# Class 0 of the long filters begun a phase earlier, and the context filter's weights requested a row ahead

## The chip, the cores and the metric

The program runs on one core of a Trainium2 chip. Times are device microseconds (us) of one execution, from start to end on the chip; a kernel's time is the median of several executions. The core has a matrix engine (TensorE, PE in the profile; its weight loads are PEld), a vector engine (DVE), a scalar engine (ACT), a general engine (POOL) and a queue that issues transfers (SP). POOL issues transfers as well. Each engine works through its own queue of instructions in order and waits at semaphores for the others.

## What is computed

Two layers of a backbone over 1024 latent tokens (a grid of 16 by 64) and 256 context tokens, model width 1024, all in float32. Layer 0 mixes tokens by a 2-D Fourier transform on half of the channels and by an order-2 Hyena operator on the other half; layer 1 is neighbourhood attention; each ends with a SwiGLU feed-forward part. The change touches layer 0's mixer:

```python
def hyena_filters(L, w1, b1, freq, w2, b2, w3):
    ...
    h = jnp.sin(freq * (z @ w1 + b1))
    h = jnp.sin(freq * (h @ w2 + b2))
    h = (h @ w3).reshape(L, 2, HY_ORDER, HY_CH)
    ...
    h = h * jnp.exp(-t01 * deltas)[:, None, None, :]
    h = h / jnp.sum(jnp.abs(h), axis=(0, 1), keepdims=True)
    fwd, bwd = h[:, 0], h[:, 1]
    return jnp.concatenate([fwd, jnp.zeros_like(fwd[:1]), bwd[:0:-1]], axis=0)

def long_conv(u, filt, skip):
    ...
    ff = jnp.fft.rfft(filt, n=2 * L, axis=0)
    ...

def mixer_ab(u, w_in, w_out, conv_w, conv_b, w1, b1, freq, w2, b2, w3, skip):
    p = u @ w_in
    y_f = fourier_mix(p[..., :FOURIER_CH])
    y_h = hyena_mix(p[..., FOURIER_CH:], conv_w, conv_b, w1, b1, freq, w2, b2, w3, skip)
    return jnp.concatenate([y_f, y_h], axis=-1) @ w_out
```

For each of two orders there is a long filter (for the 1024 latent tokens) and a context filter (for the 256 context tokens). Both are made from the same weights w3 and turned into spectra.

## The kernel before, in words

A float32 product is made of three matmuls of a reduced type: each operand is split into a high part (a cast on ACT, L349) and a low part (a subtraction on DVE, or POOL, L351). So every operand that PE needs costs one instruction on ACT and one on DVE first.

The input projection (in_proj, L1032 on) makes p = u @ w_in in 16 rows of 128 channels, in the order 0 to 9, 12 to 15, 10, 11. Its weights come from memory one row at a time (tiles ws, split into wh and wl). Between the matmuls of one row the kernel weaves other work, the piece that belongs to the row before (the function filled): how many steps of each kind stands in a tuple of numbers per row. There are three such kinds. "long" makes the long filters, "filt" the context filters, "ada" the modulation vectors (custom DVE operations, L561).

A filter of one order is made in two parts. filter_raw requests the two halves of w3 (128x512 tiles s<-in_w, on SP), makes their sum and difference (on DVE for the long filters, on POOL, L762, for the context), splits them, and multiplies on PE with the positions' features; the product is multiplied by a window loaded from memory (L786). spectrum_l (the long filters) or spectrum_c (the context) then takes the transform as matmuls with a stored matrix (tiles tk<-in_ff_l, loaded and cast).

spectrum_l goes through four classes of frequencies in the order 2, 3, 0, 1, each in two halves p, with two operands k = 0, 1 each. An operand is a tap sum or difference of the raw filter (t tiles, from L916, L917, L955, L957, L959), split into two tiles. The generator operands runs two operands ahead of the matmuls. Classes 2 and 0 need the sums (function sums): class 0's first one needs f0, a copy of the raw filter with a corrected first row (L940 to L942). PE's results are evicted by ACT (L1000) or DVE (L1009, L1011) and stored (d<-s). Where class 0 begins, PE first makes a row sum (tile c, the matmuls ps<-s,c).

Also woven in are the Fourier half's pieces: a projected row is stored to memory (d_115 and others) and read back in another layout (s<-d; d_97 is such a tile), and DVE folds it (L1484 to L1492).

The whole program is written down in program order. A framework then takes it with its own estimate of times and its pools of tiles (35 slots "s" of the S2 kind, 6 slots "t", 8 banks of PE's accumulator memory and others) and decides the order on each engine and on SP. So code that is written earlier is not necessarily executed earlier by the same amount, and a tile's slot decides when its load may go out.

Of the kernel before, what the change touches and what calls it, by code (L numbers as in the profile page):

```python
# [16 lines left out]
MUL, ADD, SUB, MAX, MIN = ALU.mult, ALU.add, ALU.subtract, ALU.max, ALU.min  # L17
# [241 lines left out]
class Builder:  # L259
# [643 lines left out]
    def spectrum_l(self, o, raw, tot):  # L903

        nc, a = self.nc, self.a
        V = nc.vector
        classes = (2, 3, 0, 1)
        fe, fo = raw[(0, 0, 0)], raw[(0, 0, 1)]
        m0, m1, m2 = (self.mask[:, k:k + 1] for k in range(3))
        fh = []  # L910

        def sums(i, k):
# [20 lines left out]
                V.tensor_tensor(u, t, u, ADD)  # L933
            return x, u

        def operands():
            for i in classes:
                if i == 0:
                    f0 = self.f0 = self.S2()
                    V.tensor_copy(f0, fe)  # L940
                    V.tensor_tensor(f0[0:1, :], fe[0:1, :], fo[0:1, :], ADD)
                    V.scalar_tensor_tensor(f0[0:1, :], f0[0:1, :], 0.5, self.taps0[o][0:1, :], op0=MUL, op1=ADD)  # L942
                even = []
                for p in (0, 1):
                    mt = self.cast2(a["ff_l"][i, p])
                    for k in (0, 1):
                        if i % 2 == 0:
                            if p == 0:
                                even.append(sums(i, k))
                            t = even[k][p]  # L950
                        else:
                            f, r = (raw[(p + 2 * k, q, i // 2)] for q in (0, 1))
                            t = self.T()
                            if i == 1 and p + k == 0:
                                V.scalar_tensor_tensor(t, r, m1, f0, op0=MUL, op1=ADD)  # L955
                            elif p + k == 0:
                                V.scalar_tensor_tensor(t, f, m0, r, op0=MUL, op1=ADD)  # L957
                            else:
                                V.tensor_tensor(t, f, r, SUB if i == 1 else ADD)  # L959
                        xh, xl = self.S2(F32R), self.S2(F32R)  # L960
                        self.split(t, xh, xl)
                        yield xh, xl, mt[k]

        ops = operands()
        ready = [next(ops), next(ops)]
        yield
        for i in classes:
            cls, eo = i % 2, i // 2
            kept = []
            for p in (0, 1):  # L970
# [22 lines left out]
                for f in (0, 1):  # L993
# [4 lines left out]
                    if cls == 0 or p == 0:  # L998
                        t = self.S2()
# [7 lines left out]
                    elif p:  # L1007
                        x, t = self.S2(), kept[f]
# [1465 lines left out]
    def run(self):  # L2474
        nc, a = self.nc, self.a
        self.setup()
        raws = {sq: ({}, {}) for sq in ("l", "c")}
# [11 lines left out]
        u = Act()  # L2489
        ng = self.first_norm(u)  # L2490
# [12 lines left out]
        def filters():  # L2503
# [3 lines left out]
            for o in (0, 1):  # L2507
# [9 lines left out]

        long = filters()
        ada = self.late_groups((2, 3), "ws")
        filt = (x for o in (0, 1) for g in (self.filter_raw("c", raws["c"], (o,)), self.spectrum_c(o, raws["c"][o]))  # L2520
                for x in g)
        self.Y = {}
        y = Act()

        def four():
            y.t.update(self.new_act(pcs=(2,), blocks=range(4)).t)
            yield from self.fourier_c(y)

        def conv():
# [4 lines left out]
            yield from self.inverse_c(1, y)  # L2534

        fc, cc = four(), conv()
        self.in_proj(u, ng, ((long, (1, 2, 4, 5, 5, 5, 5, 5, 6, 0)), (filt, (0,) * 9 + (3, 3, 3, 3, 2)),
                             (ada, (0,) * 5 + (1, 1, 2, 1, 2, 1, 2, 1, 2, 1, 2))), fc, cc)
        self.held = False
        for i in range(8):  # L2540
# [40 lines left out]
        u = None  # L2581
# [30 lines left out]
        def first_row():  # L2612
            yield from self.wino_first(h, 0, 3, rest.pop())

        first = first_row()
# [27 lines left out]
        h2, o, h4 = Act(), Act(), Act()  # L2643
# [58 lines left out]
        for i, _ in enumerate(first_part(1)):  # L2702
            if i == 7:
                c = self.rms_begin(0)
            if i == 12:
                first = self.wino_first(h2, 1, 3, self.rms_end(0, c))
            if i > 12 and i % 3 == 1:
                next(first, None)
        sums = {}
# [32 lines left out]
        c = self.rms_begin(1)  # L2742
# [87 lines left out]
```

## Time and profile before

| | |
|---|---|
| three runs | 2885.43, 2874.94, 2883.71 us (median 2883.71) |
| the profiled execution | 2878.63 us, its span 2876.9 us |
| mean granted clock of TensorE | 0.986 |
| PE busy | 2775.4 us, 96% of the span |
| DVE busy | 2078.4 us, 72% |
| ACT busy | 1314.9 us, 46% |
| POOL busy | 542.6 us, 19% |
| moved by DMA | 557.35 MB, mean 194 GB/s |

The busy share is that of the whole span. The input projection lies between about 150 and 500 us. A row of the timeline has the start, the duration, the engine, the line, the operation, what is written and read (with buffer numbers left out), the shape and how many are joined in the row; in brackets stands the idle time just before it, and what ended that.

### The profile page before, as it was taken

How to read it: one execution, taken by the hardware profiler on the slowest of the kernel's cores; microseconds unless marked ns; L12 is line 12 of the kernel's file. 1: busy time of each engine (PE TensorE's matmuls, PEld its weight loads, DVE VectorE, ACT ScalarE, POOL GpSimd, SP SyncE). 2: the span in 40 equal slices, each digit the busy share in tenths (PEclk: the TensorE clock that was granted, in tenths of full speed). 3: DMA queues.
4: the chain of work that ended last, by engine and by line, in shares of the span. 5: the costliest groups of instructions: out<-in, count | busy, mean ns of one | idle time of the engine just before them, and what ended most of it. 6: DMA issues, size and time to landing. Idle time of an engine off the chain costs nothing. (4 is left out here: it accounts for less than half of the span.)

```text
span 2876.9 us, 43752 instructions
## 1 busy us (share of the span) xinstructions
PE 2775.4 (96%) x15570; PEld 2327.5 (81%) x15570; DVE 2078.4 (72%) x3657; ACT 1314.9 (46%) x2261; POOL 542.6 (19%) x875
## 2 busy tenths in 40 slices
PE   7999888999999999999999999999999999999998
PEld 3877677887899888888888888888887788888886
DVE  5678888768787888866777536777778887764555
ACT  4434234543554333333445326777765433333433
POOL 1210234351001211222110002232221022112000
PEclk9999899999999999999999999999999999999999
DMA  7355546756566555658984436686865366435663
GB/s 263 107 163 178 167 131 193 237 170 228 204 192 213 200 200 197 211 192 330 309 310 148 146 120 161 183 196 177 238 217 203 110 249 217 153 110 177 226 190 132
DMA packets 298216, 557.35 MB, mean 194 GB/s; under 512 B 82056, under 2 KB 128330, under 8 KB 297998
## 3 DMA queue, kind: packets, MB, share of 16 engines
q1 hardware_dynamic: 234894, 367.34, 40.8%
q0 software_dynamic: 60800, 183.02, 18.1%
q10 hardware_dynamic: 2304, 4.20, 0.4%
q8 instruction: 123, 2.02, 0.3%
q14 instruction: 95, 0.78, 0.1%
HBM read 407.10 MB, written 119.80 MB: 183 GB/s over the span
## 5 line engine op out<-in xcount | busy, mean ns | idle before, releaser
L1888 PE MATMUL ps<-s,s 128*128 128x512 f32 x1976 | 489.6, 390 | 3.5 <-DVE s L351 3.1
L1888 PEld LDWEIGHTS ps<-s,s 128*128 128x128 f32 x1976 | 371.6, 188 | 81.7 <-DVE s L351 3.5
L345 PE MATMUL ps<-s,wh 128*128 128x256 f32 (+1 forms) x1784 | 408.8, 332 | 3.8 <-DVE s L786 1.8
L345 PEld LDWEIGHTS ps<-s,wh 128*128 128x128 f32 x1784 | 298.6, 191 | 38.3 <-DVE s L786 2.3
L345 PE MATMUL ps<-s,wl 128*128 128x256 f32 (+1 forms) x892 | 271.8, 330 | 1.7 <-DVE wl L351 1.6
L2065 PE MATMUL ps<-s,s 128*128 128x512 f32 (+1 forms) x1000 | 259.9, 383 | 3.5 <-DVE s L351 3.3
L349 ACT CAST s<-s 128x1024 fp32r<-128x1024 f32 (+2 forms) x192 | 172.7, 927 | 197.1 <-DMA s<-d 168.1
L351 DVE TENSOR_TENSOR wl<-ws,wh 128x1024 fp32r<-128x1024 f32 (+1 forms) x141 | 168.8, 1197 | 128.2 <-ACT wh L349 123.5
L345 PE MATMUL pq<-s,wh 128*128 128x512 f32 (+1 forms) x840 | 254.4, 384 | 0.0
L345 PE MATMUL ps<-s,s 128*128 128x65 f16 (+4 forms) x2748 | 228.4, 234 | 16.6 <-DMA s<-tk 9.4
L349 ACT CAST wh<-ws 128x1024 fp32r<-128x1024 f32 (+1 forms) x141 | 144.8, 1027 | 207.9 <-PE ps L345 90.2
L351 DVE TENSOR_TENSOR s<-s,s 128x1024 fp32r<-128x1024 f32 (+2 forms) x170 | 190.6, 1152 | 53.0 <-ACT s L349 50.5
L349 ACT CAST s<-t 128x512 fp32r<-128x512 f32 (+2 forms) x238 | 133.6, 582 | 206.8 <-PE ps L1888 72.4
L2065 PEld LDWEIGHTS ps<-s,s 128*128 128x128 f32 x1000 | 184.3, 188 | 42.3 <-DVE s L351 5.9
L351 DVE TENSOR_TENSOR s<-t,s 128x512 fp32r<-128x512 f32 (+2 forms) x238 | 150.8, 648 | 69.4 <-ACT s L349 50.5
L1888 PE MATMUL ps<-s,wh 128*128 128x512 f32 x616 | 191.7, 390 | 0.0
L345 PEld LDWEIGHTS ps<-s,wl 128*128 128x128 f32 x892 | 166.8, 190 | 19.4 <-DVE wl L351 2.5
L345 PEld LDWEIGHTS pq<-s,wh 128*128 128x128 f32 x840 | 149.0, 189 | 21.2
L345 PE MATMUL pq<-s,wl 128*128 128x512 f32 (+1 forms) x420 | 158.8, 378 | 0.0
L2065 PE MATMUL ps<-s 128*128 128x512 f32 (+1 forms) x500 | 150.9, 385 | 0.0
L345 PEld LDWEIGHTS ps<-s,s 128*128 128x128 f32 (+1 forms) x828 | 129.4, 192 | 22.7 <-issue 3.2
L336 POOL DMA_DIRECT2D d<-s x154 | 83.2, 541 | 303.8 <-DVE s L1695 94.8
(491 smaller groups left out, 5558.2 us busy)
## 6 DMA issues: line engine op xcount, KB each, us to landing
s<-d SPq DMA_DIRECT2D x283, 256.0 KB, 4.1
s<-in_down SPq DMA_DIRECT2D x150, 256.0 KB, 4.3
d<-s POOLq DMA_DIRECT2D x138, 256.0 KB, 3.5
s<-in_ada_w POOLq DMA_DIRECT2D x64, 512.0 KB, 5.0
d<-tk POOLq DMA_DIRECT2D x98, 256.0 KB, 4.2
ws<-in_up SPq DMA_DIRECT2D x44, 512.0 KB, 3.7
d<-g POOLq DMA_DIRECT2D x86, 256.0 KB, 2.8
ws<-in_gate SPq DMA_DIRECT2D x42, 512.0 KB, 3.6
```

The costliest lines, as they stand in the source:

```text
L336: self.last_ldr = self.nc.gpsimd.dma_start(out, in_).ins
L345: self.last_mm = self.nc.tensor.matmul(o, l, r, start=st, stop=sp).ins
L349: self.last_hi = nc.scalar.copy(hi, src).ins
L351: self.last_lo = eng.tensor_tensor(lo, src, hi.bitcast(F32), SUB).ins
L1888: nc.tensor.matmul(ps, x[:, sl], y, start=first and j == 0 and x is wh and y is xh, stop=j == 3 and x is wl, skip_group_check=True)
L2065: m = nc.tensor.matmul(acc[j][:, c0:c1], x[:, sl], y[:, xs], start=first and k == 0, stop=last and k == 2, skip_group_check=True)
```

## The change

Two parts of the program are written in another order. No instruction is added or removed.

Long filters. The three operations for f0 become a function, first, which is called when class 3's first half has its second operand; class 0's two sums are made one each with class 3's second half, and class 2's two sums both at the start. Before, f0 and the first sum of class 0 were made with class 0's first operand.

Context filters. The generator filt becomes ctx_filters. The request for order 0's w3 is a step of its own, and the counts of steps per row go from (0,)*9 + (3, 3, 3, 3, 2) to (0,)*8 + (1, 2, 3, 3, 3, 3). In sum over the rows: order 0's request now comes in row 8 and not 9; rows 9 to 12 end at the same step as before; rows 13 and 14 end one step and two steps further on (15 and 18 where there were 14 and 16). The condition k == 99 is never true, so order 1's request stays where it was.

```diff
+        def first():
+            f0 = self.f0 = self.S2()
+            V.tensor_copy(f0, fe)
+            V.tensor_tensor(f0[0:1, :], fe[0:1, :], fo[0:1, :], ADD)
+            V.scalar_tensor_tensor(f0[0:1, :], f0[0:1, :], 0.5, self.taps0[o][0:1, :], op0=MUL, op1=ADD)
+
         def operands():
+            even = {2: [sums(2, 0), sums(2, 1)], 0: []}
             for i in classes:
-                if i == 0:
-                    f0 = self.f0 = self.S2()
-                    V.tensor_copy(f0, fe)
-                    V.tensor_tensor(f0[0:1, :], fe[0:1, :], fo[0:1, :], ADD)
-                    V.scalar_tensor_tensor(f0[0:1, :], f0[0:1, :], 0.5, self.taps0[o][0:1, :], op0=MUL, op1=ADD)
-                even = []
                 for p in (0, 1):
                     mt = self.cast2(a["ff_l"][i, p])
                     for k in (0, 1):
                         if i % 2 == 0:
-                            if p == 0:
-                                even.append(sums(i, k))
-                            t = even[k][p]
+                            t = even[i][k][p]
...
                         yield xh, xl, mt[k]
+                        if i == 3 and p == 0 and k:
+                            first()
+                        if i == 3 and p:
+                            even[0].append(sums(0, k))
...
-        filt = (x for o in (0, 1) for g in (self.filter_raw("c", raws["c"], (o,)), self.spectrum_c(o, raws["c"][o]))
-                for x in g)
+        def ctx_filters():
+            gens = [self.filter_raw("c", raws["c"], (o,)) for o in (0, 1)]
+            next(gens[0])
+            yield
+            for o in (0, 1):
+                for _ in gens[o]:
+                    yield
+                for k, _ in enumerate(self.spectrum_c(o, raws["c"][o])):
+                    if o == 0 and k == 99:
+                        next(gens[1])
+                    yield
+
+        filt = ctx_filters()
...
-        self.in_proj(u, ng, ((long, (1, 2, 4, 5, 5, 5, 5, 5, 6, 0)), (filt, (0,) * 9 + (3, 3, 3, 3, 2)),
+        self.in_proj(u, ng, ((long, (1, 2, 4, 5, 5, 5, 5, 5, 6, 0)), (filt, (0,) * 8 + (1, 2, 3, 3, 3, 3)),
```

What became of it on the engines, at three places. The numbers behind a name are a tile's and its use's; lines after the change are higher by 3 from about L966 on.

DVE, class 0 of order 0 (t_467 and s2_469 before, t_454 and s2_456 after are its first sums). Before:

```order
L351 TENSOR_TENSOR s2_452_1643<-t_450_1640,s2_451_1642 128x512
L351 TENSOR_TENSOR s2_455_1655<-t_453_1652,s2_454_1654 128x512
L940 COPY s2_464_1690<-s4_269_944 128x512
L941 TENSOR_TENSOR s2_464_1690<-s4_269_944,g_271_949 1x512
L942 SCALAR_TENSOR_TENSOR s2_464_1690<-s2_464_1690,s2_395_1449 1x512
L916 TENSOR_TENSOR t_467_1698<-s2_464_1690,s4_269_944 128x512
L917 TENSOR_TENSOR t_468_1699<-s4_324_1168 128x512
L916 TENSOR_TENSOR t_474_1720<-s4_311_1106 128x512
L917 TENSOR_TENSOR t_475_1721<-s4_366_1332 128x512
L955 SCALAR_TENSOR_TENSOR t_502_1822<-s4_269_944,c_7_95,s2_464_1690 128x512
```

After:

```order
L938 COPY s2_448_1636<-s4_269_944 128x512
L939 TENSOR_TENSOR s2_448_1636<-s4_269_944,g_271_949 1x512
L351 TENSOR_TENSOR s2_453_1647<-t_451_1644,s2_452_1646 128x512
L940 SCALAR_TENSOR_TENSOR s2_448_1636<-s2_448_1636,s2_395_1449 1x512
L916 TENSOR_TENSOR t_454_1656<-s2_448_1636,s4_269_944 128x512
L917 TENSOR_TENSOR t_455_1657<-s4_324_1168 128x512
L958 TENSOR_TENSOR t_459_1668<-s4_368_1337 128x512
L916 TENSOR_TENSOR t_470_1706<-s4_311_1106 128x512
L917 TENSOR_TENSOR t_471_1707<-s4_366_1332 128x512
L954 SCALAR_TENSOR_TENSOR t_502_1822<-s4_269_944,c_7_95,s2_448_1636 128x512
```

The first two of f0's operations went ahead of a split of class 3 (L351), and class 3's last tap (t_459, with its split, which stands four rows below this piece) came between class 0's sums.

ACT, class 0 of order 1 (s2_689 and s2_692 before, s2_695 and s2_698 after are evictions of class 3; wh is the next projection row's weights). Before:

```order
L349 CAST s2_682_2500<-t_681_2498 128x512
L349 CAST s2_685_2512<-t_684_2510 128x512
L349 CAST wh_804_2947<-ws_803_2946 128x1024
L1000 COPY s2_689_2523<-ps_677_2492 128x512
L1000 COPY s2_692_2526<-ps_678_2493 128x512
L1026 ACTIVATE s2_703_2579<-ps_617_2305,c_93_317 128x256
```

After:

```order
L349 CAST s2_683_2504<-t_682_2502 128x512
L920 CAST s2_688_2519<-t_686_2515 1x512
L349 CAST s2_691_2528<-t_690_2526 128x512
L1003 COPY s2_695_2539<-ps_677_2492 128x512
L1003 COPY s2_698_2542<-ps_678_2493 128x512
L1029 ACTIVATE s2_709_2595<-ps_617_2305,c_93_317 128x256
L1029 ACTIVATE s2_710_2599<-ps_618_2306,c_95_319 128x512
L1029 ACTIVATE s2_711_2603<-ps_619_2307,c_95_319 128x512
L349 CAST s2_725_2643<-t_685_2514 128x512
L349 CAST wh_806_2951<-ws_805_2950 128x1024
```

The cast of the row's weights moved from ahead of the two evictions to behind them, the short convolution's activations and the split of class 0's first operand. On DVE, f0 and class 0's first sums of order 1 now stand behind class 3's splits, 21 rows further up; the last split of class 0 is row 402 of the queue and was row 403.

SP, the transfers around the context filter's order 0 (in_w3 are its weights, d_97 the Fourier half's read, d_687 to d_732 before and d_693 to d_732 after are stores of the long filters' results). Before:

```order
L330 DMA s2_784_2885<-in_cgf_c 128x128
L330 DMA d_687_2522<-s2_772_2840 128x512
L330 DMA d_690_2525<-s2_773_2845 128x512
L330 DMA d_729_2663<-s2_768_2813 128x512
L330 DMA s2_794_2899<-d_97_320 128x256
L330 DMA d_732_2669<-s2_769_2815 128x512
L330 DMA s2_809_2973<-in_w3 128x512
L330 DMA s2_810_2975<-in_w3 128x512
```

After:

```order
L330 DMA s2_774_2859<-in_w3 128x512
L330 DMA d_693_2538<-s2_772_2831 128x512
L330 DMA d_696_2541<-s2_773_2836 128x512
L330 DMA d_729_2663<-s2_768_2813 128x512
L330 DMA s2_775_2861<-in_w3 128x512
L330 DMA d_732_2669<-s2_769_2815 128x512
L330 DMA s2_786_2889<-in_cgf_c 128x128
L330 DMA s2_796_2903<-d_97_320 128x256
```

The first half of w3 took the place of in_cgf_c, the second half that of the read of d_97, which now comes last of the eight. On DVE one more operation of the modulation vectors (L561) stands between the fold of that read and L786.

More of the change, by code (lines that the diff above doesn't have):

```diff
@@ L954, in operands @@
                             if i == 1 and p + k == 0:
-                                V.scalar_tensor_tensor(t, r, m1, f0, op0=MUL, op1=ADD)
+                                V.scalar_tensor_tensor(t, r, m1, self.f0, op0=MUL, op1=ADD)
                             elif p + k == 0:
```

## The prediction

> **What bounds the kernel now.** First the head of the page, for the engine that is nearly always busy:
>
> ```profile
> span 2876.9 us, 43752 instructions
> PE 2775.4 (96%) x15570; PEld 2327.5 (81%) x15570; DVE 2078.4 (72%) x3657; ACT 1314.9 (46%) x2261; POOL 542.6 (19%) x875
> ```
>
> TensorE (PE) is busy for 2775.4 of 2876.9 us: only 101 us of idle time are left in the whole program, and whatever the change brings must come out of those, or out of stretches at a low clock. So the next view is a table by stretches, to see where those 101 us lie:
>
> ```profile
> core 0: us, PE busy (x) PEld busy (x) DVE busy (x) ACT busy (x) POOL busy (x), PEclk, DMA share, GB/s
> 100.00:200.00 100.00, 95.56 (x490) 77.19 (x488) 77.64 (x158) 39.73 (x81) 20.66 (x34) 0.95 0.46 152
> 200.00:300.00 100.00, 93.70 (x442) 74.06 (x441) 81.23 (x159) 40.33 (x67) 9.00 (x17) 0.98 0.54 177
> 300.00:400.00 100.00, 87.00 (x423) 70.48 (x422) 78.10 (x186) 29.88 (x62) 28.40 (x37) 0.93 0.54 165
> 400.00:500.00 100.00, 88.94 (x433) 73.95 (x434) 86.38 (x163) 44.81 (x80) 36.51 (x30) 0.91 0.53 169
> 800.00:900.00 100.00, 100.00 (x878) 99.76 (x877) 73.05 (x92) 51.64 (x72) 10.81 (x20) 1.00 0.66 210
> ```
>
> From 800 us on PE has no gap; from 100 to 500 us, where the input projection runs with the filters woven into it, it idles 34.8 us and its clock is 0.91 to 0.98. The change lies in these 400 us alone. The third view is PE's timeline there, for its gaps (in brackets: idle us before the row, and what ended it):
>
> ```profile
> 158.19 1.65 PE L345 MATMUL ps<-s,tk 128*128 128x512 f32 x4 [0.25 <-DVE s L351]
> 193.25 2.25 PE L345 MATMUL ps<-s,c 128*2 128x512 f32 x4 [3.80 <-ACT s L349]
> 204.94 0.40 PE L345 MATMUL ps<-s,wh 128*128 128x256 f32 x2
> 294.80 0.39 PE L345 MATMUL ps<-s,c 128*2 128x512 f32 x1 [2.15 <-ACT s L349]
> 308.95 1.66 PE L345 MATMUL pq<-s,tk 128*128 128x512 f32 x6 [0.85 <-ACT s L1000]
> 312.05 1.67 PE L345 MATMUL ps<-s,tk 128*128 128x512 f32 x6 [1.45 <-DMA tk<-in_ff_l]
> 317.80 1.52 PE L345 MATMUL ps<-s,tk 128*128 128x512 f32 x6
> 319.16 0.87 PE L345 MATMUL ps<-s,wh 128*128 128x256 f32 x4
> 328.62 0.39 PE L345 MATMUL ps<-s,wl 128*128 128x512 f32 x1
> 332.03 0.50 PE L345 MATMUL ps<-g,s 128*128 128x512 f32 x1 [3.03 <-ACT g L349]
> 335.02 0.80 PE L345 MATMUL ps<-s,s 128*128 128x256 f32 x2 [2.37 <-DVE s L351]
> 340.32 0.79 PE L345 MATMUL ps<-s,wh 128*128 128x256 f32 x2 [1.83 <-DVE s L786]
> 448.71 0.70 PE L345 MATMUL ps<-s,tk 128*128 128x512 f32 x1 [1.79 <-ACT s L349]
> 460.35 1.12 PE L1241 MATMUL ps<-c,s 128*128 128x128 f32 x4 [3.03 <-DVE s L351]
> ```
>
> 193.25 and 294.80 are the starts of class 0 in orders 0 and 1 of the long filters; 332.03 to 340.32 is the context filter's order 0; 448.71 and 460.35 are the end of the projection. Every gap ends on a cast (ACT), a subtraction (DVE) or an eviction of a small chain, so the fourth view is DVE's timeline, ahead of those places:
>
> ```profile
> 157.45 0.68 DVE L351 TENSOR_TENSOR s<-t,s 128x512 fp32r<-128x512 f32 x1
> 158.05 0.68 DVE L917 TENSOR_TENSOR s<-s 128x512 f32<-128x512 f32 x1
> 179.56 1.29 DVE L351 TENSOR_TENSOR s<-t,s 128x512 fp32r<-128x512 f32 x2 [7.29 <-ACT s L349]
> 180.77 0.44 DVE L940 COPY s<-s 128x512 f32<-128x512 f32 x1
> 193.23 0.69 DVE L351 TENSOR_TENSOR s<-t,s 128x512 fp32r<-128x512 f32 x1
> 282.68 1.23 DVE L351 TENSOR_TENSOR wl<-ws,wh 128x1024 fp32r<-128x1024 f32 x1 [1.50 <-ACT wh L349]
> 283.82 0.42 DVE L940 COPY s<-s 128x512 f32<-128x512 f32 x1
> 299.72 0.67 DVE L351 TENSOR_TENSOR s<-t,s 128x512 fp32r<-128x512 f32 x1
> 326.50 0.29 DVE L1484 TENSOR_TENSOR t<-s 128x127 f32<-128x127 f32 x1 [5.20 <-DMA s<-d]
> 331.09 0.78 DVE L561 CUSTOM_DVE_ANT_0 t<-ws,s,c 128x512 f32<-128x512 f32 x1
> 339.58 0.68 DVE L786 TENSOR_TENSOR s<-ps,s 128x512 f32<-128x512 f32 x1
> ```
>
> From 180.77 to 193.23 DVE makes f0 and class 0's taps, sums and splits without a pause, 20 instructions, and PE starts 0.02 us behind the last split's start. The same chain runs from 283.82 to 299.72 in order 1. From 326.50 to 339.58 DVE is busy without a pause as well.
>
> **The change, place by place.** No instruction is added or taken away on any engine; only places in the queues move. The sum is therefore made of differences at five places. A gain is positive.
>
> Place 1, start of order 0 (158 us). Class 2's second sums now come ahead of the first operand, so three more DVE operations stand before the split of 157.45 (L917, L926 and L957). From one start to the next such an operation takes 0.60 us (157.45 to 158.05), so the split comes 1.8 us later, and PE, which waited 0.25 us for it already, loses 1.8 us. Ends: 0 (if what these three did later on is missed there) and -1.8. I take -1.8.
>
> Place 2, class 0 of order 0 (193 us). Two of the chain's 20 instructions, L940 and L941, now stand ahead of the wait that ends at 179.56 and run inside its 7.29 idle us. But class 3's last tap and split, two instructions that before were over by 180.8, come into the middle of the chain. So the chain's end hardly moves. What changes is the gap's form: PE waits first for class 3's late operand, then works six matmuls on it, and then waits for class 0. With 0.6 us a step I place these at 1.4 and 1.3 us in place of 3.80: a gain of 1.1. The clock is a second term: between 193.25 and 204.94 PE ran 34 matmuls in 11.7 us. At full rate six take 1.36 us (317.80 to 319.16), so 34 take 7.7: 4.0 us were lost to a low clock. With two shorter gaps this can vanish (4.0) or stay (0). I take half, 2.0, since between 332 and 340 gaps of 3.03, 2.37 and 1.83 us, none as long as 3.80, stand in a stretch of clock 0.93. Place 2 gives +3.1, between -1 (chain later, clock as before) and +7.8 (the gap and the low clock both gone).
>
> The Trainium skill (TensorE: Matmul & The Clock Gate, "What's actually happening") says that the clock is halved after an idle window of about 3.4 us and restored after as much sustained work. The 3.80 us gap with slow matmuls behind it agrees; by that rule two gaps of 1.4 and 1.3 us would cost no clock at all, the clock term would be 4.0 in place of 2.0, and the sum below 2.0 us better.
>
> Place 3, class 0 of order 1 (295 to 313 us). ACT and the queue show why DVE began late:
>
> ```profile
> 281.60 1.05 ACT L349 CAST wh<-ws 128x1024 fp32r<-128x1024 f32 x1 [1.58 <-DMA ws<-in_w_in]
> 283.93 1.07 ACT L1000 COPY s<-ps 128x512 f32<-128x512 f32 x2 [1.29 <-DVE wl L351]
> ```
>
> The cast of the next projection row's weights waited for its load until 281.60; the evictions L1000 stood behind it, and on DVE the weights' second half (282.68) stood ahead of f0. Now this cast stands behind the evictions on ACT, and f0 and class 0's first sums stand right behind class 3's splits, ahead of the weights' half on DVE. Freed of that wait, the chain's start is some 4 us earlier, but eight modulation operations (L561, 0.78 us at 331.09) that stood ahead of the chain now stand in its middle, so the last class 0 split comes about 1.4 us earlier than 299.72. The next row's matmuls also now stand ahead of class 1's second half, which covers the waits of 0.85 and 1.45. The sum is 3.7; I take +3.5. Ends: 0, and the idle before 294.80, 308.95 and 312.05 altogether, 4.5, with what row matmuls fill besides: 6.
>
> Place 4, the context filter's order 0 (328 to 340 us). Here the request is meant to lead by a row. The queues of SP and POOL before:
>
> ```profile
> 313.48 0.37 SPq L330 DMA_DIRECT2D s<-in_cgf_c  x1
> 321.14 0.45 SPq L330 DMA_DIRECT2D s<-d  x1
> 322.21 0.96 SPq L330 DMA_DIRECT2D s<-in_w  x2
> 330.06 2.95 POOL L762 TENSOR_TENSOR t<-s,s 128x512 f32<-128x512 f32 x2 [2.95 <-DMA s<-in_w]
> DMA packets 2576, 3.39 MB, mean 261 GB/s; under 512 B 279, under 2 KB 1564, under 8 KB 2576
> ```
>
> In the new order the first half of w3 takes the place of in_cgf_c (313.48), 8.7 us ahead. But the second half takes the place of the Fourier read s<-d (321.14), which leads by only about a microsecond, since both stand behind a store that waits for the row's evictions. Both halves are needed for L762. The read of d_97 now stands behind the second half, a store and in_cgf_c: 256 + 256 + 64 KB, which at the 261 GB/s of 318 to 331 us (last row) take 2.2 us. Its reader L1484 is the head of DVE's queue from 326.50, and everything to L786 at 339.58 stands behind it without a pause, now with one L561 more (0.7). So L786 comes 2.9 us later against the row's end, and PE's 11.7 us from 328.62 to 340.32 become 14.6: I take -2.9, a loss. w3 itself, earlier by about a microsecond, brings nothing, because DVE is the last to arrive. Ends: +1 (the read isn't late, and the L762 sum lets g come sooner), and -9.5 (below, second rival).
>
> Place 5, the end (440 to 465 us). Steps 15 to 18 of the context filter come a row earlier, so the operand for which PE waited 1.79 us at 448.71 is ready. The 3.03 us at 460.35 hang on casts and splits that stand behind a load and don't move. DVE is busy for 86.38% from 400 to 500 us, so the time is only partly kept: +1.0, between -1 and +4. Order 1's weights are still requested in the row that uses them (the branch k == 99 is never reached): 0. After about 700 us the queues are the same.
>
> The sum is -1.8 + 3.1 + 3.5 - 2.9 + 1.0 = 2.9 us of gain. The profiled execution took 2878.63 us, so by its own time the changed kernel would take 2875.7. The median of the three runs, 2883.71, is 5.1 us above it, so against it I forecast 2880.8, or 2881.
>
> **The rivals.** First, the stalls do go. Place 2 yields its 7.8, place 3 its 6, place 5 its 4, and the read is only the one L561 later (-0.7), with place 1 at 0: 17 us, 2866 to 2867, faster by 0.6%. For it speaks that places 2 and 3 are gaps whose releaser is begun earlier; against it that DVE is 78 to 86% busy between 300 and 500 us and passes a lead on only where it has a gap.
>
> Second, slower: SP blocks at the second half of w3. That row waits for PE to release its tile. If this comes only with the row's last matmul (328.62) and not around 322, d_97 follows at about 329.9 (three requests of 0.4 to 0.5 us later) and lands 5.4 us after that (326.50 less 321.14), at 335.3: 8.8 us late. With the L561, place 4 then costs 9.5; with place 1 and nothing from the others, 11.3 us: 2895. It decides against the forecast once the read lands over 5 us late, and reaches 0.5% (14.4 us) when it is 12 us late, or 9 late with the in_win_c loads behind it as late as itself. For it speaks that SP's queue goes in order, so that one late slot holds up all behind it; against it that the read that had this place went out at 321.14, directly behind the stores.
>
> Third, the change does not do what it says: the slots hand the moved operations their old places. Then the time is 2884, give or take 4. For it speaks that the last class 0 split of order 1 is now row 402 of DVE's queue, and was row 403; against it that ACT's and SP's queues have changed ahead of it.
>
> **How the numbers follow.** My forecast (2874 to 2888, the five terms at or between their middle values) has a chance of 0.50, the first rival 0.18, the second 0.22, the third 0.10. A difference of 0.5%, 14.4 us, is about what a measurement of this kernel can tell from none (its three runs spread over 10.5 us). The first rival lies under 2869.3 in 0.14 of its 0.18, with 0.02 from the forecast's tail: faster 0.16. The second lies over 2898.1 in 0.14 of its 0.22, with 0.02 from other tails: slower 0.16. The rest, 0.68, is the same. The range reaches to the middle of the two rivals, 2867 to 2897.
>
> **What the new profile would show.** Place 1: PE idles about 2 us near 158. Place 2: two gaps under 2 us in place of 3.80 near 193, and six 128x512 matmuls in some 1.4 us directly behind them if the clock stays. Place 3: no wait for tk<-in_ff_l behind class 0 of order 1, and the row after it begins 3 us earlier. Place 4: the first in_w request near in_cgf_c's old time, the second within 2 us of 322; DVE's first L1487 2 us later against the row's end; 14 to 15 us from that end to the matmul released by L786. If that figure is under 11 or over 18 the fourth term is wrong. Place 5: no gap on a cast near 449. The forecast is wrong if DVE's lead at places 2 and 3 is worth nothing, or if PE keeps full clock throughout and the table's rows from 100 to 500 us rise by more than 10 us of busy time.

## The result: slower by 0.7%

The changed kernel took 2899.88 us (median; 2898.22 to 2903.41), the one before, run beside it, 2879.32 us. The ratio is 1.0073, 95% interval 1.0053 to 1.0094: 21 us slower, between 15 and 27. The head of its profile and the same stretches as before:

```profile
span 2897.0 us, 43757 instructions
PE 2777.9 (96%) x15570; PEld 2331.7 (80%) x15570; DVE 2084.1 (72%) x3657; ACT 1316.6 (45%) x2261; POOL 545.3 (19%) x875
```

```profile
core 0: us, PE busy (x) PEld busy (x) DVE busy (x) ACT busy (x) POOL busy (x), PEclk, DMA share, GB/s
100.00:200.00 100.00, 94.98 (x486) 77.31 (x485) 77.41 (x158) 39.55 (x80) 20.73 (x34) 0.95 0.45 148
200.00:300.00 100.00, 91.75 (x437) 73.43 (x435) 77.49 (x152) 39.16 (x64) 8.50 (x16) 0.98 0.53 167
300.00:400.00 100.00, 81.03 (x362) 63.37 (x363) 73.36 (x164) 27.17 (x56) 23.85 (x33) 0.84 0.50 151
400.00:500.00 100.00, 84.68 (x423) 70.47 (x423) 80.65 (x176) 39.00 (x72) 29.61 (x26) 0.91 0.54 173
```

The work is the same. PE idles 47.6 us in the four stretches from 100 to 500 us, where it was 34.8, and between 300 and 400 us its granted clock fell from 0.93 to 0.84. PE's timeline of the changed kernel at the prediction's places:

```profile
159.88 2.93 PE L345 MATMUL ps<-s,tk 128*128 128x512 f32 x6 [0.41 <-DVE s L351]
193.42 0.39 PE L345 MATMUL ps<-s,c 128*2 128x512 f32 x1 [1.46 <-ACT s L349]
195.72 1.33 PE L345 MATMUL ps<-s,c 128*2 128x512 f32 x3 [1.16 <-DVE s L351]
300.47 0.59 PE L345 MATMUL ps<-s,c 128*2 128x512 f32 x1 [1.97 <-DVE s L351]
332.82 0.39 PE L345 MATMUL ps<-s,wl 128*128 128x512 f32 x1
340.12 0.79 PE L345 MATMUL ps<-g,s 128*128 128x512 f32 x1 [6.92 <-ACT g L349]
350.17 0.63 PE L345 MATMUL ps<-s,wh 128*128 128x256 f32 x2
392.12 0.49 PE L345 MATMUL ps<-s,tk 128*128 128x512 f32 x1 [1.49 <-ACT s L349]
418.00 0.79 PE L345 MATMUL ps<-g,s 128*128 128x512 f32 x1 [3.20 <-ACT g L349]
```

Against the kernel before, the row's end (328.62) is 4.2 us later, the matmuls freed by L786 (340.32) are 9.9 later, and order 1's first matmul of the context weights (401.79 before) is 16.2 later. By 653 us the lag is 20.0, and at the end of the span it is 20.1. So the time went in three portions: 4 us up to the row's end, 6 at the context weights of order 0, 6 from there to those of order 1; some 4 more come up to 653 us. These are differences between two traces, and the first portion is the least certain: ten of the kernels below have PE's order of the kernel before up to the row's end, and in their traces that end lies up to 5.3 us later than in its trace. In the six kernels with the change's long filters it lies 4.2 to 7.1 us later. The next two views show the second portion, on SP and on DVE:

```profile
317.85 0.33 SPq L330 DMA_DIRECT2D s<-in_w  x1
325.13 0.42 SPq L330 DMA_DIRECT2D s<-in_w  x1
326.12 0.48 SPq L330 DMA_DIRECT2D s<-in_cgf_c  x1
326.69 0.39 SPq L330 DMA_DIRECT2D s<-d  x1
```

```profile
334.37 0.29 DVE L1487 TENSOR_TENSOR t<-s 128x127 f32<-128x127 f32 x1 [9.08 <-DMA s<-d]
349.23 0.67 DVE L786 TENSOR_TENSOR s<-ps,s 128x512 f32<-128x512 f32 x1
```

The read of d_97 goes out last, 5.5 us later than before, and lands 7.7 us after its request (5.4 before). Its reader starts 1.6 us behind the start of the row's last matmul, where it was 2.1 us ahead. From there to L786 DVE takes 14.9 us in place of 13.1.

The third portion was in no step of the prediction. Two things differ there. The first is on DVE and POOL, in the kernel before:

```profile
373.86 1.70 POOL L1128 TENSOR_TENSOR t<-s,s 128x512 f32<-128x512 f32 x1 [2.62 <-DVE s L1029]
374.36 1.75 DVE L858 SCALAR_TENSOR_TENSOR t<-s,c,s 128x512 f32<-128x512 f32 x1
375.52 1.74 POOL L860 TENSOR_TENSOR t<-s,s 128x512 f32<-128x512 f32 x1
377.21 0.57 POOL L336 DMA_DIRECT2D tk<-in_ff_c  x1
377.80 0.76 POOL L1132 TENSOR_TENSOR s<-t 128x256 f32<-128x256 f32 x1
```

and in the changed kernel:

```profile
386.32 0.58 POOL L336 DMA_DIRECT2D tk<-in_ff_c  x1 [3.04 <-PE ps L345]
386.60 4.76 DVE L858 SCALAR_TENSOR_TENSOR t<-s,c,s 128x512 f32<-128x512 f32 x1
386.92 1.28 POOL L1131 TENSOR_TENSOR t<-s,s 128x512 f32<-128x512 f32 x1
388.15 1.29 POOL L860 TENSOR_TENSOR t<-s,s 128x512 f32<-128x512 f32 x1
389.40 0.73 POOL L1135 TENSOR_TENSOR s<-t 128x256 f32<-128x256 f32 x1
390.09 0.72 POOL L1136 TENSOR_TENSOR s<-t 128x256 f32<-128x256 f32 x1
```

POOL's request for a matrix (tk) now stands ahead of its four operations, and had stood in their middle. The four run one behind the other from 386.92 to 390.81, and DVE's L858, which makes an operand of the context filter's spectrum, ends only at 391.36: 4.76 us in place of 1.75. PE waits for that operand at 392.12. This wait is called the hold below. DVE as a whole loses little by it: L858 and the two 128x256 operations behind it took 5.2 us before (374.36 to 379.55) and take 5.4 us now (386.60 to 392.03), because before the change those two were the slow ones.

The Trainium skill (SBUF — State Buffer, "SBUF: two separate sides") says that DVE and POOL share one pair of memory ports, that whichever issues first holds it for a whole instruction and that the other blocks. The rows agree that one of the two blocks. They don't agree on which: by the recorded starts L858 was first (386.60 against 386.92), and it ended behind four POOL operations in a row, in the kernel before behind one.

The second thing is the order of what follows. The context filter's spectrum has a second operand, whose split (L351) now stands behind seven of the modulation operations (L561) counted from L858, where it stood behind four. Its matmuls, with tk, stand behind the first matmuls of the next projection row. Their result is evicted and stored, and a later read for the Fourier half (not that of d_97) comes behind that store on SP. Before:

```profile
383.21 0.68 DVE L351 TENSOR_TENSOR s<-t,s 128x512 fp32r<-128x512 f32 x1
383.21 1.47 PE L345 MATMUL ps<-s,tk 128*128 128x512 f32 x4 [1.05 <-DVE s L351]
385.98 0.44 SPq L330 DMA_DIRECT2D s<-d  x1
391.62 0.54 DVE L1484 TENSOR_TENSOR t<-s 128x127 f32<-128x127 f32 x1
401.79 0.49 PE L345 MATMUL ps<-g,s 128*128 128x512 f32 x1 [2.41 <-ACT g L349]
```

After:

```profile
397.59 0.69 DVE L351 TENSOR_TENSOR s<-t,s 128x512 fp32r<-128x512 f32 x1
401.52 0.62 PE L345 MATMUL ps<-s,tk 128*128 128x512 f32 x2
403.28 0.37 SPq L330 DMA_DIRECT2D s<-d  x1
407.83 0.29 DVE L1487 TENSOR_TENSOR t<-s 128x127 f32<-128x127 f32 x1 [4.51 <-DMA s<-d]
```

Counted from the matmuls freed by L786, this read is requested at 53.1 us in place of 45.7 and folded on DVE at 57.7 in place of 51.3. Order 1's first context matmul follows the fold by 10.2 us in both kernels. POOL's sum of order 1's w3 (L762) stands behind a subtraction that waits for operations behind the fold on DVE (it starts at 397.69 before, 413.92 after). So the third portion goes by the lateness of this later read.

### The profile page after: what moved, and what is told of

It is laid out like the page before. It is cut to its first block, busy times and chain, and to the rows that moved or that the text cites. A ratio compares the mean times of both kernels' runs of the same rounds, so it can differ in the third digit from the quotient of the medians.

```text
span 2897.0 us, 43757 instructions
## 1 busy us (share of the span) xinstructions
PE 2777.9 (96%) x15570; PEld 2331.7 (80%) x15570; DVE 2084.1 (72%) x3657; ACT 1316.6 (45%) x2261; POOL 545.3 (19%) x875
## 5 line engine op out<-in xcount | busy, mean ns | idle before, releaser
L1891 PEld LDWEIGHTS ps<-s,s 128*128 128x128 f32 x1976 | 371.6, 188 | 81.7 <-DVE s L351 3.5
L351 DVE TENSOR_TENSOR wl<-ws,wh 128x1024 fp32r<-128x1024 f32 (+1 forms) x141 | 168.6, 1196 | 121.1 <-ACT wh L349 116.4
L351 DVE TENSOR_TENSOR s<-s,s 128x1024 fp32r<-128x1024 f32 (+2 forms) x170 | 190.7, 1152 | 50.7 <-ACT s L349 50.6
L2068 PEld LDWEIGHTS ps<-s,s 128*128 128x128 f32 x1000 | 184.4, 188 | 41.2 <-DVE s L351 4.9
L351 DVE TENSOR_TENSOR s<-t,s 128x512 fp32r<-128x512 f32 (+2 forms) x238 | 152.2, 653 | 76.5 <-ACT s L349 56.3
L345 PEld LDWEIGHTS ps<-s,s 128*128 128x128 f32 x835 | 130.4, 192 | 22.4 <-issue 2.6
```

The lines of the kernel that those rows point to most:

```text
L345: self.last_mm = self.nc.tensor.matmul(o, l, r, start=st, stop=sp).ins
L351: self.last_lo = eng.tensor_tensor(lo, src, hi.bitcast(F32), SUB).ins
L1891: nc.tensor.matmul(ps, x[:, sl], y, start=first and j == 0 and x is wh and y is xh, stop=j == 3 and x is wl, skip_group_check=True)
L2068: m = nc.tensor.matmul(acc[j][:, c0:c1], x[:, sl], y[:, xs], start=first and k == 0, stop=last and k == 2, skip_group_check=True)
```

## The experiments

Each kernel is given with its ratio to the kernel before of its own comparison; us are that ratio on 2879 us.

**The parts apart.** e1_long has the new spectrum_l and the old filt; e2_ctx the opposite. e3_request and e4_tail divide e2_ctx by its counts:

```diff
-(filt, (0,) * 9 + (3, 3, 3, 3, 2))
+(filt, (0,) * 8 + (1, 2, 3, 3, 3, 2))     e3_request, with ctx_filters
+(filt, (0,) * 9 + (3, 3, 3, 3, 3))        e4_tail
```

> The long filters' part alone; the context filter as before. Theory A (the request that displaces the Fourier read is the cause): +2 to +5 us against the kernel before, that is the 2.5 us lost at 167 us and the 2.2 us lost up to the row's end at 329 us, and from DVE's first fold (L1487) to L786 the 13.1 us of before. Theory B (class 0's new order and the clock stretches it causes are the cause, the late read only an echo): +12 us or more, with PE at half clock for over 10 us more between 290 and 420 us.

Measured: 1.0010 (0.9996 to 1.0025), +3 us.

> The context filter's part alone (request a row ahead and the new counts); the long filters as before. Theory A: +14 to +18 us, with the read of d_97 landing 7 to 8 us after its request and PE's stretch from the row's end to the L786 matmuls 16 to 17 us in place of 11.7. Theory B: +2 to +6 us.

Measured: 1.0057 (1.0038 to 1.0076), +16 us.

> Only the request of order 0's w3 a row ahead; the steps of rows 13 and 14 as before. Theory A in its narrow form (the late read alone): +6 to +12 us, with 5.5 us of it between the row's end and L786. If e2_ctx is slow and this is not, the steps 15 to 18 that come a row earlier are the cause. Theory B: +1 to +4 us.

Measured: 1.0035 (1.0014 to 1.0056), +10 us. PE's end of the row, and the matmuls freed by L786:

```profile
328.66 0.39 PE L345 MATMUL ps<-s,wl 128*128 128x512 f32 x1
346.54 0.63 PE L345 MATMUL ps<-s,wh 128*128 128x256 f32 x2
```

> Only the counts of rows 13 and 14 raised to three steps each, so that steps 15 to 18 come a row earlier; request and long filters as before. Theory A: -2 to +2 us. If the end of the projection (444 to 502 us, 57.3 us before and 58.7 us after the change, and 61.3 and 64.0 us up to 563 us) is where the tail's steps cost, +3 to +6 us.

Measured: 1.0003 (0.9989 to 1.0018), +1 us.

The context filter's request is most of the loss. Moved alone it stretches the 11.7 us after the row's end to 17.9, with the row ending where it did before. The tail's steps are worth nothing that can be told, and the long filters' part is at most a small loss (-1 to +7 us). Theory B, which held class 0 and its clock responsible, falls.

**The read put back, or made late by itself.** e5_read_first and e8_both_read_first leave the request in row 8, but behind the Fourier step, in e2_ctx and in the whole change:

```diff
             if i > 7:
                 todo.append(four)
+            if i == 8:
+                todo.remove(fill[1][0])
+                todo.append(fill[1][0])
```

> The context filter's part alone as in e2_ctx, but in row 8 the request for w3 is made after the Fourier step, so that the read of d_97 keeps its old place on SP, ahead of w3. Theory A (the read that comes late is the cause): -2 to +4 us against the kernel before, where e2_ctx had +16. Theory C (not the read, but the order of the context filter's operations on DVE, ACT and PE and the steps that come a row earlier): +12 to +18 us, as e2_ctx.

Measured: 1.0014 (1.0000 to 1.0028), +4 us in place of +16.

> The whole change, but in row 8 the request for w3 stands after the Fourier step as in e5_read_first. Theory A: 0 to +6 us, what is left being the long filters' part (e1_long, +2). Theory C: +15 to +21 us, as the changed kernel.

Measured: 1.0019 (1.0008 to 1.0030), +5 us in place of +21. In both, SP's order there is that of the kernel before, so w3 is no earlier either; they undo the place and show that it was the cause, but not yet which consequence of it. e6_store2 and e7_store4 are the kernel before with two and four more stores (n) of a finished tile in front of the read:

```diff
                         self.ld(self.frg[("l", o, 1, f)][eo], x)
+                        if o == 1 and i == 1 and f == 0:
+                            for _ in range(n):
+                                self.ld(self.DR([P, HC]), x)
```

> The kernel before with two more stores of 256 KB (to a place that nobody reads) ahead of the read of d_97; filters and request as before. Theory A: the read lands 3 to 5 us later against the row's end and the time rises by 5 to 12 us, about as much as e3_request (+11.5). Theory C: 0 to +3 us.

Measured: 1.0018 (1.0005 to 1.0032), +5 us. The fold starts 0.1 us behind the start of the row's last matmul, 2.2 us later than in the kernel before, less than the 3 to 5 us that were expected.

> The same with four such stores. Theory A: the read 7 to 10 us later, the time up by 10 to 20 us, so the price of a late read is 1.5 to 2.5 us for each us. Theory C: 0 to +4 us.

Measured: 1.0003 (0.9992 to 1.0014), +1 us. In its trace the read is as late as in the changed kernel: the fold 2.3 us behind the row's last matmul, and L786's matmuls 17.5 us behind it.

```profile
330.76 0.39 PE L345 MATMUL ps<-s,wl 128*128 128x512 f32 x1
348.23 0.80 PE L345 MATMUL ps<-s,wh 128*128 128x256 f32 x2 [1.78 <-DVE s L786]
```

```profile
333.04 0.29 DVE L1487 TENSOR_TENSOR t<-s 128x127 f32<-128x127 f32 x1 [9.59 <-DMA s<-d]
382.69 1.77 DVE L858 SCALAR_TENSOR_TENSOR t<-s,c,s 128x512 f32<-128x512 f32 x1
```

This was against Theory A: the same loss at the place, but hardly any at the end (-2 to +4 us). The profiled execution is 7.9 us late at 348 us, 7.1 late at order 1's weights, 4.6 at 653 us and 0.6 at its end, so in this one trace the later stages take it up. In e3_request, 6.2 us at the first place had grown to 13.0 at order 1's weights. L858 takes 1.77 us here and 4.78 there. So there is a second cause between the two places, and the held L858 was the candidate that the next runs were made for.

**The held operation.** e11_sub_dve is e3_request with one POOL operation of the four (L860, order 0) on DVE; e13_before_sub_dve does that to the kernel before, as control, and e14_change_sub_dve to the changed one.

```diff
-                    nc.gpsimd.tensor_tensor(t, f, r, SUB)
+                    (nc.gpsimd if o else nc.vector).tensor_tensor(t, f, r, SUB)
```

> As e3_request with the read late, but the subtraction L860 of order 0 is made on DVE, so that POOL runs one operation less in a row there. If the 4.8 us hold on DVE's L858 (four POOL operations in a row) is a part of e3_request's loss: L858 under 3 us and a time 2 to 5 us below e3_request's, +6 to +9 us. If it is only seen there and costs nothing: +10 to +13 us.

Measured: 1.0017 (1.0006 to 1.0027), +5 us, a little under the +6 to +9 expected if the hold is a part of the loss. The read is nearly as late as in e3_request (17.2 us from the row's end to L786's matmuls, 17.9 there); no DVE operation there is over 2.2 us, and L858 takes 1.22.

> The kernel before with the subtraction L860 of order 0 on DVE; nothing else changed. The control to e11_sub_dve: if the hold on DVE's L858 is what that edit removed, the edit alone is worth nothing here, -2 to +2 us. If the edit is a gain of its own: -3 us or better, and e11_sub_dve says nothing of the hold.

Measured: 0.9998 (0.9988 to 1.0008): the edit alone is worth nothing that can be told.

> The whole change with L860 of order 0 on DVE. If the hold is a part of the change's loss: +10 to +16 us in place of about +20, and no operation of DVE near 386 us over 3 us. If not: +18 to +22 us.

Measured: 1.0029 (1.0017 to 1.0041), +8 us in place of +21, more of a gain than was expected, though the first loss is all there (L786's matmuls 11.3 us later than before). L858 takes 1.91 us.

The time between two rows of each PE timeline, L786's matmuls of order 0 and the first context matmul of order 1, separates the kernels. The third column has the fold of that later read, counted from the first of the two rows, the fourth the L561 operations between L858 and the second operand's split:

| kernels | us between the two | fold at | L561 ahead of the split | longest DVE operation, us |
|---|---|---|---|---|
| before | 61.5 | 51.3 | 4 | 2.1 |
| the change, e2_ctx, e3_request | 67.8, 67.9, 68.3 | 57.7, 57.7, 58.1 | 7 | L858, 4.8 |
| e18_long_late_sum_read_early (below) | 66.0 | 56.1 | 7 | L1135, 4.4 |
| e7_store4, e10_read_pool, e9_w3_pool (read late, no hold) | 60.6, 59.6, 62.0 | 50.4, 49.4, 51.7 | 5, 4, 5 | 2.0 to 2.1 |
| e11_sub_dve, e14_change_sub_dve (read late, hold removed) | 59.9, 60.2 | 48.6, 48.9 | 1, 1 | 2.2, 1.9 |
| e13_before_sub_dve | 59.8 | 49.7 | 1 | 2.1 |

The late read moves the start of this stretch and not its length. What makes it 6 to 8 us longer is not separated by these runs. The hold and the split behind seven L561 come together, in the same four kernels of the twenty, and the edit of e11_sub_dve and e14_change_sub_dve removed both: with L860 on DVE the planner (the framework that decides the order) put the split behind one L561 and its matmuls ahead of the next row's. In all twenty the first context matmul of order 1 follows the fold by 9.9 to 11.3 us, so the length goes by the later read, and that goes by the order. A kernel with this order and without the hold, or the other way round, wasn't run.

**Other ways to the read and w3.** e9_w3_pool and e12_change_w3_pool send order 0's w3 by POOL's queue in e3_request and in the change, e10_read_pool the first read by POOL's queue in e3_request:

```diff
-                self.ld(st[(o, j)], a["w3"][:, (2 * j + o) * HC:(2 * j + o + 1) * HC])
+                (self.ldr if sq == "c" and o == 0 else self.ld)(
+                    st[(o, j)], a["w3"][:, (2 * j + o) * HC:(2 * j + o + 1) * HC])
...
-                self.ld(p, self.pd[k])
+                (self.ld if k else self.ldr)(p, self.pd[k])
```

> As e3_request (order 0's w3 requested a row ahead), but the two loads go out on POOL's queue, so that SP keeps the read of d_97 where it was before and w3 is really early. If w3's lateness cost the kernel before anything (the change's idea), -3 to -9 us against the kernel before, with DVE's stretch from the fold to L786 under 13 us. If DVE is the last to arrive there (the prediction's reading), -1 to +4 us, although w3 lands several us before L762 needs it.

Measured: 1.0026 (1.0014 to 1.0038), +7 us. The aim was missed: POOL's queue waited for DVE, the two loads went out at 321.11 (322.21 in the kernel before), and the read was late again (fold at 330, L786's matmuls 16.8 us behind the row). So no kernel here has w3 early, and what that would bring isn't tried.

> As e3_request with w3 on SP where the change puts it, but the read of d_97 goes out on POOL's queue, so that w3 no longer stands ahead of it; POOL's request for a matrix then stands behind the subtraction L860 again, as in the kernel before. Theory A (late read, and the order that the planner makes of it): 0 to +4 us, and the hold of 4.8 us on DVE's L858 near 383 us is gone (1.8). If w3's own place on SP costs (two tile slots held a row longer): +8 to +13 us, as e3_request.

Measured: 1.0009 (0.9994 to 1.0024), +3 us. The read landed late in POOL's queue too (fold at 333.90, 2.4 us behind the row's last matmul), but L858 took 1.77 us. So it repeats e7_store4: late read, no hold, and little loss (-2 to +7 us).

> The whole change with w3's two loads on POOL's queue. Theory A: 0 to +7 us, as e8_both_read_first (+5.5 by the ratio), in place of the +21 of the change.

Measured: 1.0038 (1.0025 to 1.0050), +11 us, more than the 0 to +7 expected. It is about the sum of e9_w3_pool (+7) and e1_long (+3).

**The read early.** e15_read_early starts the Fourier step a row earlier and lets it stop once behind the first read; e16_change_read_early does so in the changed kernel.

```diff
-            if i > 7:
+            if i > 6:
                 todo.append(four)
...
                 self.ld(p, self.pd[k])
+                if k == 0:
+                    yield
```

> The kernel before with the read of d_97 requested a row ahead (and nothing else ahead). If the read sets the context filter's start, DVE's first fold comes 3 to 5 us earlier against the row's end (2.1 us ahead of it in the kernel before), PE's stretch from the row's end to the L786 matmuls falls from 11.7 to 7 to 9 us, and the time by 2 to 6 us. If w3's arrival then sets it: 0 to -1 us, with the same stretch.

Measured: 0.9987 (0.9975 to 0.9999), -4 us: faster than both kernels, at the edge of what can be told. The fold is done at 305.00, PE's gaps after the row's end sum to 3.6 us in place of 7.2, and L786 sets the last of them:

```profile
332.96 0.39 PE L345 MATMUL ps<-s,wl 128*128 128x512 f32 x1
339.51 0.79 PE L345 MATMUL ps<-s,wh 128*128 128x256 f32 x2 [2.58 <-DVE s L786]
```

> The whole change with the read of d_97 a row ahead as well, so that w3's first half and the read both lead. If the read's lateness and what the planner made of it are all of the change's loss: -6 to +3 us, the stretch after the row's end under 9 us. If w3's tile slots or class 0's order cost by themselves: +6 to +12 us.

Measured: 1.0007 (0.9996 to 1.0018), +2 us in place of +21. L858 takes 1.78 us, and the second operand's split stands behind four L561 again. With the read early, the second and third portions are gone.

**Class 0 by itself.** e17_long_late_sum is e1_long with class 2's second sums back at their operand, e18_long_late_sum_read_early adds the early read.

```diff
-            even = {2: [sums(2, 0), sums(2, 1)], 0: []}
+            even = {2: [], 0: []}
...
+                            if i == 2 and p == 0:
+                                even[2].append(sums(2, k))
```

> The long filters' part alone as in e1_long, but class 2's second sums are made at the second operand again, as before the change. If the 2.7 us that PE lost near 159 us come from those three operations ahead of the first split: the gap near 157 us is 0.25 us again, and the row that starts at 166.8 us (before) starts within 0.5 us of that in place of 2.2 us later. The time against the kernel before: 0 to -3 us if class 0's earlier operands are worth something once this is undone, 0 to +3 us if the order of class 0 gains nothing by itself.

Measured: 1.0002 (0.9991 to 1.0014). The row that began at 169.31 in the changed kernel begins at 167.12, as before within 0.3 us:

```profile
159.10 1.18 PE L345 MATMUL ps<-s,tk 128*128 128x512 f32 x4 [0.26 <-DVE s L351]
167.12 0.48 PE L345 MATMUL ps<-s,wh 128*128 128x256 f32 x2 [0.18 <-DVE s L1033]
```

So the sums at the start cost what place 1 said, and class 0's new order brings nothing by itself that can be told (-3 to +4 us).

> The same with the read of d_97 a row ahead as in e15_read_early. If the two are independent: the sum of e17_long_late_sum and of e15_read_early (-3.7), so -4 to -7 us or about -1 us; a version that could beat both kernels. If DVE, busy 80%, passes on nothing of class 0's lead: as e15_read_early, -2 to -5 us.

Measured: 1.0009 (0.9998 to 1.0021), +3 us, where the two parts apart sum to -3. Its trace has the hold once more, on another DVE operation, with POOL's request again ahead of the same four operations:

```profile
373.55 4.38 DVE L1135 TENSOR_TENSOR s<-t 128x256 f32<-128x256 f32 x1
```

```profile
373.15 0.57 POOL L336 DMA_DIRECT2D tk<-in_ff_c  x1 [3.59 <-DVE t L1132]
373.75 1.27 POOL L1133 TENSOR_TENSOR t<-s,s 128x512 f32<-128x512 f32 x1
```

The stretch of the table is 66.0 us in it, like the other kernels with a hold, although its first read is early. So this loss doesn't need the late first read. But L858 took 0.74 us here, its result was there 35.2 us behind the row freed by L786 (35.8 in the kernel before), and the first operand's split came at 42.7 (42.2 before). The second split, behind seven L561, came at 45.4 (42.9), its matmuls at 47.4 (43.6), the read's request at 51.5 (45.7) and the fold at 56.1 (51.3). So in this kernel nearly all of the longer stretch comes from the order.

## Why the prediction was wrong

By the traces, places 1 to 4, which were to gain 1.9 us together, lost 9.9; 6.4 us more were lost where the sum had no term, and some 4 behind that.

**Place 1** held: predicted 1.8 us of loss, 2.5 measured at 169.31 against 166.81, and gone in e17_long_late_sum. From 150 to 167 us the six kernels with these sums at the start lose 1.4 to 3.0 us, the others nothing.

**Place 2** was right on the gaps, wrong on their worth. Two gaps of 1.4 and 1.3 us were forecast, 1.46 and 1.16 came (and one of 0.47). Of the 3.1 us gain 0.4 came, because the clock was halved just as long, 6.8 us in both kernels. The step that failed is the half of the clock term. The whole clock loss, taken as 4.0 us there, was too large as well: 6.8 us at half clock can't have cost more than 3.4. Cut into the 3.41 us windows in which the clock changes, the changed kernel shows:

```profile
192.59:196.01 3.42, 1.30 (x5) 0.65 (x5) 3.42 (x6) 1.66 (x3) 0.00 (x0) 1.00 0.62 161
196.01:199.42 3.41, 2.94 (x8) 1.60 (x8) 3.32 (x7) 0.00 (x0) 0.00 (x0) 0.51 0.57 223
199.42:202.83 3.41, 3.41 (x9) 2.27 (x8) 0.00 (x0) 0.00 (x0) 0.00 (x0) 0.50 0.42 159
```

(columns as in the tables by stretches: PE busy comes first behind the length, PEclk third from the end). A window in which PE was busy for 1.30 of 3.42 us is followed by half clock; no gap need last 3.4 us. By the Trainium skill's rule (TensorE: Matmul & The Clock Gate, "What's actually happening"), as the prediction took it, two gaps of that size would cost no clock: the trace differs.

**Place 3** was forecast at +3.5 us and came out at -2.1 (behind place 2 the lag is 2.1 us, at the row's end 4.2). By single traces the size is rough: the other kernels with a new order of class 0 lose 3.1 to 6.0 us there, and the ten that keep the old order up to the row's end 0.4 to 4.0. The wait for tk<-in_ff_l went away as forecast. But the chain of class 0 was stretched by the operations that moved into its middle, so that PE waited for DVE at three rows (1.93, 1.55 and 1.97 us, up to 300.47), and half clock lasted 10.2 us between 290 and 313 us in place of 3.4. e17_long_late_sum says of the whole order that it is worth nothing that can be told.

**Place 4** had the right mechanism and sign: the read behind w3, L786 behind the read. The term was too small, 2.9 against 5.7 us. The read came 3.7 us later against the row's end, not 2.2: three requests ahead of it take their time on SP as well, and it took 7.7 us to land, not 5.4. DVE's stretch grew by 1.8 us, not 0.7. The second rival, the late read, lay nearest (2895). But its price was carried to the end as if nothing took it up; by e7_store4 (+1 us) and e10_read_pool (+3) it is taken up in good part when nothing else changes, by e6_store2 (+5) and e9_w3_pool (+7), whose reads are also late, less. Where in the later stages, isn't settled.

**Place 5**, +1.0 us, isn't seen; e4_tail says +1, between -3 and +5.

**What had no step at all** is the largest: the 6.4 us between order 0's context weights and order 1's. The prediction took the queues of SP, DVE and ACT up to the row freed by L786, looked at POOL's for L762 alone, and put everything from there to 440 us at nothing. The runs showed two changes there. A request of 0.57 us, moved on POOL's queue, made four POOL operations run without a pause, and DVE's L858 took 4.76 us in place of 1.75. And the second operand's split moved behind three more L561 and its matmuls behind the next row's, so that the later read, its fold and order 1's context matmuls came 6 to 7 us later. The stretch is 66.0 to 68.3 us in the four kernels with both, against 59.6 to 62.0 in the sixteen others (the kernel before among them).

With both of these removed the change loses 8 us in place of 21 (e14_change_sub_dve, 0.44%, 13 us, the intervals apart), and e3_request 5 in place of 10 (e11_sub_dve, 0.18%, 5 us, the intervals overlap). So that this stretch costs is shown, the size lies somewhere in between, and how it is divided between the hold and the order stays open; e18_long_late_sum_read_early speaks for the order.

## What to carry to other kernels

A request moved ahead on an in-order queue takes the place of what stood there; before counting its gain, look at what now comes last and who heads the next engine's queue behind it. When a planner decides the order, compare all queues of the two kernels from the change onward, those of engines that are hardly busy too, and not only at the places that were meant to move: here one split and its matmuls moved back by a few places, and a read that stood behind their store went late. When an edit cures a loss, look at what else it moved before naming the cause. A gain at a gap is worth only what the engine that feeds it can pass on: DVE made class 0's operands without a pause, and a better order of them brought nothing that can be told.

## What was not expected of the hardware

Half clock can follow a window of 3.41 us in which PE was busy in part. At class 0 it followed windows with 0.03 and 1.26 us of PE in the kernel before, and with 1.30 and 0.80 in the changed one:

```profile
189.43:192.84 3.41, 0.03 (x1) 0.00 (x0) 3.41 (x6) 0.45 (x2) 0.00 (x0) 1.00 0.38 90
291.83:295.24 3.41, 1.26 (x6) 0.62 (x4) 3.41 (x7) 0.62 (x1) 0.00 (x0) 1.00 0.75 231
```

Over the whole of these two traces half clock begins 30 times, 23 times behind a window with 1.7 us of PE or less; some windows with 1.6 us or more were followed by full clock as well, so the border isn't sharp. The busy share isn't all: the others are the end of each program and five windows with 2.5 to 3.4 us of PE, in each of which small matmuls ran (of 128x1, of 2x2 or of one row). No such border shows for the way back: full clock followed windows at half clock with 2.84 to 3.41 us of PE, and half clock went on behind one with 3.41. Busy times of PE are modelled at their ends, so these shares are rough.

The other surprise is the hold: a DVE operation that took 1.22 us in e11_sub_dve, recorded as begun 0.3 us ahead of POOL's first, ended after POOL's fourth.
